# A two-layer decoder trunk with a searched order of issue: the order searched anew, the sinks' load on SyncE's queue, the first weight row in two transfers, and tile 0's output ahead of tile 1's

## The chip, the cores and the metric

The kernel runs on one core of one Trainium2 chip. The metric is the device time of one execution, in microseconds (us). The engines are called as in the profile: PE (TensorE matmul) with PEld (its weight loads), DVE (VectorE), ACT (ScalarE), POOL (GpSimd) and SP (SyncE, which here only issues transfers).

## The reference

256 tokens of width 1024 go through two layers and a last norm. Each layer is conditioned by a vector c: a shift, a scale and a gate come from it by a product with a matrix of 1024 x 3072.

```python
c_act = jax.nn.silu(c)
for layer in range(DEPTH):
    ada = jnp.einsum('bd,de->be', c_act, w_ada[layer]) + b_ada[layer]
    shift, scale, gate = jnp.split(ada, 3, axis=-1)
    h = rms_norm(x, norm_g[layer]) * (1.0 + scale[:, None, :]) + shift[:, None, :]
    ...
        y = even_mixer(h, w_in_even[i], w_out_even[i], a_sinks[i], ...)
        y = odd_mixer(h, w_in_odd[i], w_out_odd[i], cos, sin)
    x = x + gate[:, None, :] * y
return rms_norm(x, final_g)
```

Layer 0 (even) projects h to the heads of two attentions, one over a sliding window with a learned sink per head (`a_sinks`, eight numbers), one sparse in three branches. Layer 1 (odd) is a block-sparse attention. All is fp32.

## The kernel before

**Precision.** Each large product is made of three matmuls (`mm3`): both operands are split into a rounded part (hi) and a rest (lo), and hi x hi, hi x lo and lo x hi are added in PSUM. So each weight tile that lands in `raw` (a ring of five) is cast by ACT into `whi`, and DVE subtracts to get `wlo`; only then can PE use it. For the first layer `hhi`, `hlo` are the same two parts of the conditioned input h.

**Order.** No scheduler decides the order. Every call on an engine is first recorded by `Plan`, and then `issue` issues all of them in the order of a table, `ORDER` (3092 numbers in before, found by a search). Each engine works through its own calls in that order, and a call waits for what it depends on while all behind it on its engine wait too. A transfer's place in SP's order is thus its place in SP's queue. As all calls are issued at one line, every row of the profile shows L257, and operations are told apart by engine and tile.

**The opening.** The steps around the change, by their lines of before:

- The loads of x (`xs`, one transfer of 512 KB for each of two tiles of 128 tokens) and small tables; c comes in as `crow`, and `cz` holds its activated form, made on DVE out of `tiny`.
- The norm of x for each tile t, then eight transposes on PE, copied by DVE and ACT into `bigA` (`xT`).
- `start_ada` and `start_sums` (L710, L722). The weights of the projection are taken in eight rows of 128 of the 1024 inputs, and a row can begin when its shift and scale are known. So the conditioning matrix is read in pieces, for two rows at a time (`START`): eight transfers of 256 KB into the tiles `qT` (six) and `gate` (two) for rows 0 and 1, into the four tiles `t` for rows 2 and 3, and so on in turn. For the first pair PE sums all of it by 32 matmuls of 128 x 128 (`ps_m<-qT,cz` and `ps_m<-gate,cz`, two records each in the profile). For later pairs DVE sums a part (`acc`), and PE the rest (`ps_m<-t,cz`, `ps_m<-acc,ones`). ACT copies the sum (`asb`), PE transposes it, and two adds on DVE give `shs`.
- `start_row` (L767) loads a weight row into `raw`: 1304 columns (652 KB) and 384 columns (192 KB). `start_prep` (L773) makes `hhi` on ACT and `hlo` on DVE for this row and splits the weights. `start_mm` (L781) runs 24 matmuls for the row, 3 each of 512, 408, 512 and 256 columns for two token tiles, into seven PSUM banks that collect over all eight rows (`ps_s`, `ps_pj`, `ps_o`, `ps_pt`).
- The sinks (L814) are spread to 128 partitions, 32 bytes each, by one transfer of 4 KB on GpSimd's queue. DVE negates them; they are first used in an attention at 73 us. `rows` takes in `b_ada` and `norm_g`, also on GpSimd's queue; DVE needs them for `shs`.

**The middle** (from about 28 to 212 us) holds the other rows, the first layer's attentions with the conditioning of the rest, the output projection and the second layer's beginning.

**The tail.** The last product is made in pieces: columns 0 to 511 and then, for tile 0, the rest in one piece, for tile 1 in two. When a tile is complete, its norm is a root on ACT, a reciprocal on DVE, and two scalings into `t`: ACT's of 384 columns, sent from ACT's queue, and DVE's of 640, sent from SP's.

Of the kernel before, what the change touches and what calls it, by code (L numbers as in the profile page):

```python
# [13 lines left out]
P = 128  # L14
# [254 lines left out]
def tile_trunk(  # L269
# [24 lines left out]
    V, A, G, T, Y = plan.vector, plan.scalar, plan.gpsimd, plan.tensor, plan.sync  # L294
# [408 lines left out]
    W0 = w_in_even[0]  # L703
# [669 lines left out]
```

## Time and profile before

| what | value |
|---|---|
| time of a run: median of 3 (lowest to highest) | 306.07 us (305.75 to 307.39) |
| span of the profiled execution | 305.1 us |
| granted PE clock, mean | 0.997 |
| busy PE, DVE, ACT | 289.9, 260.4, 187.1 us |
| moved by transfers | 71.82 MB, mean 235 GB/s |

The span runs from the first to the last instruction of one execution; of that execution the profile gives no other time. A row of a timeline gives the start, the time, the engine, line and operation, the tiles as out<-in, the shape, how many were joined, and in brackets the idle time before it with what ended it. Rows with SPq, ACTq or POOL DMA are issues of transfers, not the transfers. Some tiles carry numbers in the order of issue (`qT0`, `qT1`) that the profile leaves out.

### The profile page before, as it was taken

The page shows a single profiled execution, that of the slowest core. Times are in us where ns is not written, and L with a number is a line of the kernel's source. Part 1 is how long each engine was busy: PE and PEld are TensorE (multiplying, and loading weights), DVE is VectorE, ACT ScalarE, POOL GpSimd, SP SyncE. Part 2 cuts the span into 40 slices and gives each one's busy share as a digit, 9 for nine tenths or more (in the row PEclk, how much of TensorE's full clock was granted, in tenths as well). Part 3 has the DMA queues.
Part 4 walks back from the last instruction along what each step waited for, and adds up shares of the span by engine and source line. Part 5 has one row for each costly group of instructions (what it writes and reads, how often), then busy time and mean ns, then how long its engine had stood idle before and what let it go on. Part 6 is the DMA issues. An engine that isn't in the chain of part 4 may idle for free.

```text
span 305.1 us, 6309 instructions
## 1 busy us (share of the span) xinstructions
PE 289.9 (95%) x2303; PEld 247.7 (81%) x2303; DVE 260.4 (85%) x706; ACT 187.1 (61%) x487; POOL 10.7 (4%) x34
## 2 busy tenths in 40 slices
PE   3969999999999999999999999999999999999991
PEld 2848888897888777877877799999789989887791
DVE  0377998999999999999999679697685999999983
ACT  4364446885687888974547753655376357685522
POOL 6000000001000000000011000000000000000010
PEclk9999999999999999999999999999999999999998
DMA  7999999989496668699799805948099673172003
GB/s 188 374 391 383 387 398 373 330 260 305 133 347 203 197 201 269 215 299 356 215 332 363 263 2 168 355 167 272 6 308 305 175 249 138 12 268 69 2 0 138
DMA packets 60669, 71.82 MB, mean 235 GB/s; under 512 B 2712, under 2 KB 52320, under 8 KB 60640
## 3 DMA queue, kind: packets, MB, share of 16 engines
q1 hardware_dynamic: 60032, 70.90, 69.7%
q0 software_dynamic: 160, 0.05, 0.5%
q10 hardware_dynamic: 448, 0.48, 0.4%
q8 instruction: 18, 0.29, 0.4%
q14 instruction: 11, 0.09, 0.1%
HBM read 70.38 MB, written 1.05 MB: 234 GB/s over the span
## 4 chain that ended last, share of the span: by engine, by line
PE 85%; DMA 9%; DVE 2%; ACT 1%; SPq 1%; issue 0%; ACTq 0%; DVEq 0%
PE ps_pj L257 51%; PE ps_s L257 12%; PE ps_o L257 7%; PE ps_pt L257 7%; PE ps_m L257 6%; DMA raw<-in_w_ada_dram 3%; DMA raw<-in_w_in_even_dram 3%; DMA qT<-in_w_ada_dram 2%; SPq L257 1%; DVE acc L257 1%; ACT whi L257 1%; DVE wlo L257 1%; ACT t L257 0%; DVE xs L257 0%; DVE sm L257 0%
## 5 line engine op out<-in xcount | busy, mean ns | idle before, releaser
L257 ACT CAST whi<-raw 128x512 fp32r<-128x512 f32 (+1 forms) x132 | 74.7, 600 | 34.9 <-PE ps_pj L257 17.5
L257 DVE TENSOR_TENSOR wlo<-raw,whi 128x512 fp32r<-128x512 f32 (+1 forms) x116 | 73.2, 659 | 3.6 <-ACT whi L257 3.2
L257 PE MATMUL ps_pj<-hlo,whi 128*128 128x256 f32 x256 | 71.8, 286 | 0.0
L257 PE MATMUL ps_pj<-hhi,wlo 128*128 128x256 f32 x256 | 71.7, 288 | 0.0
L257 PE MATMUL ps_pj<-hhi,whi 128*128 128x256 f32 x256 | 71.4, 290 | 0.1
L257 PEld LDWEIGHTS ps_pj<-hlo,whi 128*128 128x128 f32 x256 | 47.9, 188 | 2.2 <-issue 2.0
L257 PEld LDWEIGHTS ps_pj<-hhi,wlo 128*128 128x128 f32 x256 | 47.9, 189 | 0.6 <-issue 0.5
L257 PEld LDWEIGHTS ps_pj<-hhi,whi 128*128 128x128 f32 x256 | 47.3, 188 | 1.2 <-issue 0.6
L257 DVE SCALAR_TENSOR_TENSOR acc<-raw,cz,acc 128x512 f32<-128x512 f32 x42 | 31.4, 748 | 0.3
L257 ACT ACTIVATE sm<-sm,mn 128x128 f32<-128x128 f32 (+1 forms) x58 | 26.1, 452 | 5.6 <-DVE mn L257 5.6
L257 PE MATMUL ps_pj<-whi,hhi 128*128 128x512 f32 (+2 forms) x72 | 26.5, 381 | 1.5 <-ACT hhi L257 1.5
L257 DVE SCALAR_TENSOR_TENSOR wlo<-raw,whi 128x512 fp32r<-128x512 f32 x32 | 21.2, 686 | 7.7 <-ACT whi L257 7.7
L257 PE MATMUL ps_pj<-wlo,hhi 128*128 128x512 f32 (+2 forms) x72 | 26.6, 372 | 0.0
L257 PE MATMUL ps_pj<-whi,hlo 128*128 128x512 f32 (+2 forms) x72 | 26.3, 367 | 0.0
L257 PE MATMUL ps_pj<-whi,ghi 128*128 128x512 f32 (+1 forms) x56 | 20.8, 373 | 0.0
L257 PE MATMUL ps_pj<-wlo,ghi 128*128 128x512 f32 (+1 forms) x56 | 20.7, 370 | 0.0
L257 PE MATMUL ps_pj<-whi,glo 128*128 128x512 f32 (+1 forms) x56 | 20.4, 364 | 0.0
L257 ACT COPY pT<-ps_pt 128x384 f32<-128x384 f32 x25 | 11.9, 477 | 10.7 <-PE ps_pt L257 10.6
L257 PE MATMUL ps_pt<-ta,sm 128*128 128x128 f32 x87 | 18.4, 275 | 0.0
L257 PEld LDWEIGHTS ps_pj<-whi,hhi 128*128 128x128 f32 x72 | 13.3, 189 | 4.2 <-ACT hhi L257 2.0
L257 PEld LDWEIGHTS ps_pj<-wlo,hhi 128*128 128x128 f32 x72 | 13.6, 188 | 2.5 <-issue 0.4
L257 PEld LDWEIGHTS ps_pj<-whi,hlo 128*128 128x128 f32 x72 | 13.6, 189 | 2.0 <-DVE hlo L257 0.2
(235 smaller groups left out, 606.1 us busy)
## 6 DMA issues: line engine op xcount, KB each, us to landing
raw<-in_w_in_odd_dram SPq DMA_DIRECT2D x16, 1024.0 KB, 6.9
raw<-in_w_ada_dram SPq DMA_DIRECT2D x28, 512.0 KB, 6.9
raw<-in_w_in_even_dram SPq DMA_DIRECT2D x8, 652.0 KB, 7.2
raw<-in_w_in_even_dram SPq DMA_DIRECT2D x5, 1024.0 KB, 10.1
t<-in_w_ada_dram SPq DMA_DIRECT2D x16, 256.0 KB, 6.7
raw<-in_w_out_even_dram SPq DMA_DIRECT2D x4, 1024.0 KB, 6.2
raw<-in_w_out_odd_dram SPq DMA_DIRECT2D x4, 1024.0 KB, 7.0
qT<-in_w_ada_dram SPq DMA_DIRECT2D x12, 256.0 KB, 7.2
```

Source lines behind the costliest of these rows:

```text
L257: self.ops.append(dict(key=eng.key, deps=deps, fn=lambda: getattr(real, name)(*args, **kw)))
```

## The change

1. `ORDER` is another table, with 3093 numbers. Calls up to about 212 us stand in another order on each engine, displaced by some four places on PE and DVE in the mean; behind that both orders are the same up to the tail.
2. Row 0's transfer of 1304 columns is made as two, of 512 and 792 columns. The other rows keep one.
3. The sinks' load goes from GpSimd's queue to SP's.

```diff
 ORDER = [int(i) for i in """
-0 2 8 997 10 23 29 1 3 22 510 73 4 76 78 30 77 31 7 5 79 74 32 33 58 11 6 80 12 992 13 27 43 75 14 15 92 16 44
+0 2 8 3 78 74 998 993 73 10 4 58 59 5 22 11 1 23 76 80 6 32 511 29 31 75 79 77 12 7 60 28 62 25 26 61 83 24 30
...
     def start_row(g):
         raw = sb([P, 2048], "raw", RAW)
-        Y.dma_start(raw[:, 0:1304], W0[g * P : (g + 1) * P, 1152:2456])
+        for a, b in ((0, 512), (512, 1304)) if g == 0 else ((0, 1304),):
+            Y.dma_start(raw[:, a:b], W0[g * P : (g + 1) * P, 1152 + a : 1152 + b])
         Y.dma_start(raw[:, 1304:1688], W0[g * P : (g + 1) * P, 256:640])
...
     snk = const([P, 16], "snk")
-    G.dma_start(snk[:, 0:8], a_sinks[0:1, :].to_broadcast([P, 8]))
+    Y.dma_start(snk[:, 0:8], a_sinks[0:1, :].to_broadcast([P, 8]))
```

SP's queue in the opening, before: both tiles of x, the eight conditioning tiles of the first pair, then `raw0` (row 0) and `raw1` (row 1).

```order
L257 DMA xs_61<-in_x_dram 128x1024 x2
L257 DMA qT0_97<-in_w_ada_dram 128x2x256
L257 DMA qT1_98<-in_w_ada_dram 128x2x256
L257 DMA qT2_99<-in_w_ada_dram 128x2x256 x2
L257 DMA gate_76<-in_w_ada_dram 128x2x256
L257 DMA qT0_97<-in_w_ada_dram 128x2x256
L257 DMA gate_76<-in_w_ada_dram 128x2x256
L257 DMA qT1_98<-in_w_ada_dram 128x2x256
L257 DMA raw1_101<-in_w_in_even_dram 128x384
L257 DMA raw0_100<-in_w_in_even_dram 128x1304
L257 DMA raw0_100<-in_w_in_even_dram 128x384
L257 DMA raw1_101<-in_w_in_even_dram 128x1304
```

And now, from the second tile of x on; ahead of it stand the first tile of x and three conditioning tiles.

```order
L257 DMA xs_61<-in_x_dram 128x1024
L257 DMA qT1_98<-in_w_ada_dram 128x2x256
L257 DMA gate_76<-in_w_ada_dram 128x2x256
L257 DMA snk_116<-in_a_sinks_dram 128x8
L257 DMA qT1_98<-in_w_ada_dram 128x2x256
L257 DMA gate_76<-in_w_ada_dram 128x2x256
L257 DMA qT2_99<-in_w_ada_dram 128x2x256
L257 DMA raw0_100<-in_w_in_even_dram 128x384
L257 DMA raw0_100<-in_w_in_even_dram 128x792
L257 DMA t40_86<-in_w_ada_dram 128x2x256 x2
L257 DMA raw0_100<-in_w_in_even_dram 128x512
L257 DMA raw1_101<-in_w_in_even_dram 128x1304
```

The second tile of x stands behind three conditioning tiles, the sinks in the midst of them; row 0 comes ahead of row 1, its narrow columns first, and two tiles of the second pair's conditioning (`t40`) ahead of its first 512 columns.

PE in the opening, before: the sums of the first pair in one run, behind the last transposes of x, then row 0 (`whi_108`, `wlo_112` are its 1024 wide columns, `whi_109` the narrow ones; `whi_110` is of row 1).

```order
L257 MATMUL ps_s_91<-ta,t_87 128x128
L257 MATMUL ps_m_67<-qT_97,cz 32x128 x8
L257 MATMUL ps_m_67<-qT_98,cz 32x128 x8
L257 MATMUL ps_m_67<-qT_99,cz 32x128 x8
L257 MATMUL ps_m_67<-gate,cz 32x128 x8
L257 MATMUL ps_m_67<-ta,asb_106 128x128
L257 MATMUL ps_pj_94<-whi_108,hhi 128x512
...
L257 MATMUL ps_s_91<-whi_108,hlo 128x512
L257 MATMUL ps_s_90<-whi_110,hhi 128x512
L257 MATMUL ps_o_96<-whi_109,hhi 128x408
```

PE now, from the last sums that stand among the transposes of x on.

```order
L257 MATMUL ps_m_67<-qT_98,cz 32x128 x4
L257 MATMUL ps_s_90<-ta,t_87 128x128 x3
...
L257 MATMUL ps_pt_83<-ta,rows_pe 128x32
L257 MATMUL ps_m_67<-qT_99,cz 32x128 x4
L257 MATMUL ps_m_67<-gate,cz 32x128 x4
L257 MATMUL ps_s_91<-ta,t_87 128x128
L257 MATMUL ps_m_67<-ta,asb_106 128x128
L257 MATMUL ps_s_91<-ta,t_87 128x128
L257 MATMUL ps_pt_83<-whi_109,hhi 128x256
L257 MATMUL ps_o_96<-whi_109,hhi 128x408
```

24 of the 32 sums stand ahead, between the transposes, and eight behind them; `cz`, which they need, is DVE's fifth call now and stood tenth before. Row 0 begins with the narrow columns, and the first matmul of row 1 comes after 21 matmuls of row 0, where it came after 13.

ACT in the tail, before (`t_86` is tile 1's output here, `t_87` tile 0's; `parts<-parts` is the root, `t_88,parts<-xs` the square of a piece).

```order
L257 ACTIVATE parts<-parts 128x1
L257 ACTIVATE t_88,parts<-xs 128x256
L257 ACTIVATE parts<-parts 128x1
L257 ACTIVATE t_86<-xs,parts 128x384
L257 DMA out_dram<-t_86 128x384
L257 ACTIVATE t_87<-xs,parts 128x384
L257 DMA out_dram<-t_87 128x384
```

And now:

```order
L257 ACTIVATE parts<-parts 128x1
L257 ACTIVATE t_87<-xs,parts 128x384
L257 DMA out_dram<-t_87 128x384
L257 ACTIVATE t_88,parts<-xs 128x256
L257 ACTIVATE parts<-parts 128x1
L257 ACTIVATE t_86<-xs,parts 128x384
L257 DMA out_dram<-t_86 128x384
```

Tile 0's scaling and its transfer stand right behind tile 0's root, ahead of tile 1's last square, in place of the very end.

258 rows, old and new, of the table ORDER are left out of this document.

## The prediction

> **What bounds the kernel now.** I read the clock first, then the page's busy shares, the table by stretches, the chain of waits, and last the opening, one place of the middle and the tail instruction by instruction.
>
> ```profile
> core 0: 305.1 us, clock 0.997
> PE 289.9 (95%) x2303; PEld 247.7 (81%) x2303; DVE 260.4 (85%) x706; ACT 187.1 (61%) x487; POOL 10.7 (4%) x34
> 100.00:130.00 30.00, 30.00 (x273) 23.38 (x271) 29.03 (x110) 25.80 (x84) 0.00 (x0) 1.00 0.65 213
> ```
>
> The clock is full, so nothing is to be had there. The columns of a stretch are its length, then the busy time of PE, of its weight loads, DVE, ACT and POOL, the clock, the DMA share and GB/s. PE has no idle time in this one, and DVE is busy 97% of it. So in the middle neither engine has much to give, and time can be won only before that stage, by beginning it sooner, or after the last matmul. The chain of waits says the same: behind 21.7 us it is PE almost all the way, and ahead of it stand two transfers.
>
> ```profile
> PE 85%; DMA 9%; DVE 2%; ACT 1%; SPq 1%; issue 0%; ACTq 0%; DVEq 0%
> ...
> 3.38 7.24 DMA qT<-in_w_ada_dram
> ...
> 10.64 8.84 DMA raw<-in_w_in_even_dram
> ...
> 19.50 1.14 ACT whi L257 x2
> ```
>
> The profiled execution has a span of 305.1 us; the median of the three runs shown is 306.07, 0.97 above it. I make the sum as a difference to the span and put it on the median.
>
> **Opening: the sums and the first weight row.**
>
> ```profile
> 6.34 0.76 SPq L257 DMA_DIRECT2D qT<-in_w_ada_dram  x1
> DMA to landing us min/median/max: 6.8/7.3/7.7
> 13.18 1.60 PE L257 MATMUL ps_m<-qT,cz 128*32 128x128 f32 x48
> 14.60 0.62 PE L257 MATMUL ps_m<-gate,cz 128*32 128x128 f32 x16
> 15.31 0.27 ACT L257 COPY asb<-ps_m 128x128 f32<-128x128 f32 x1 [0.33 <-PE ps_m L257]
> 16.19 0.16 DVE L257 TENSOR_TENSOR shs<-shs,rT 128x2 f32<-128x2 f32 x1
> 16.82 0.60 ACT L257 ACTIVATE hhi<-bigA,shs 128x256 fp32r<-128x256 f32 x1
> 17.47 0.73 PE L257 MATMUL ps_pj<-whi,hhi 128*128 128x512 f32 x2 [1.51 <-ACT hhi L257]
> 21.70 0.49 PE L257 MATMUL ps_s<-whi,hhi 128*128 128x512 f32 x1 [1.06 <-ACT whi L257]
> ```
>
> The last of the eight conditioning tiles is issued at 6.34 us and, with the median of the qT loads, lands at about 13.6. Only then can the sums of the first two rows end, but PE begins all 64 of their matmul records at 13.18 and ends them at 15.22, 1.6 us behind the landing. The change interleaves them with the transposes of x as tiles land and leaves eight instructions for the end, shown in the order of issue as two rows of four; 64 records took 2.04 us, so a quarter of them is 0.5 us. That ends the sums 1.1 us sooner. Of the rest up to 17.47 (2.25 us: copy, transpose, two adds, hhi) nothing is removed; two weight casts on ACT stand ahead of hhi in both orders, now of the narrow columns that come first. I take 1.0 for the start of row 0, with bounds of 0.5 (ACT is late) and 1.5.
>
> Before, PE ran 13 of row 0's 24 matmuls, then waited 1.06 us at 21.70 for a cast of row 1's weights, of the transfer that the chain shows landing at 19.48. Now 21 of the 24 come first. They outlast that landing, so this wait goes: another 1.06 on PE. But the next thing is late then:
>
> ```profile
> 13.73 6.13 SPq L257 DMA_DIRECT2D t<-in_w_ada_dram  x5
> 20.61 0.34 SPq L257 DMA_DIRECT2D raw<-in_w_in_even_dram  x1
> L257 PE MATMUL ps_m<-t,cz x32: 272/273/297, 25.3 to 26.1; 128*32 128x128 f32 x32
> 27.45 0.69 DVE L257 TENSOR_TENSOR wlo<-raw,whi 128x512 fp32r<-128x512 f32 x1 [1.84 <-ACT whi L257]
> ```
>
> The second conditioning group needs its t tiles; the last is issued by 19.86, and with the shortest landing of the t loads (5.1, below) it lands at about 24.6. The group's matmuls began at 25.3, so they can begin at most about 0.7 sooner. Of the 2.06 won up to there the rest isn't all lost, since PE does matmuls of row 1 meanwhile that it has to do anyhow. Of DVE's wait of 1.84 (row 2's cast came behind asb on ACT) about half should go, and DVE is the engine without slack behind it. I take **-1.1** for the whole opening at equal transfer rate, nearer to the 0.7 than to the 2.06, and bounds of -0.3 (DVE holds it) and -2.1.
>
> ```profile
> DMA to landing us min/median/max: 5.1/8.2/8.4
> ```
>
> The first row's wide transfer becomes two, one issue more on SP. SP issues such a transfer in 0.34 us (20.61) and then mostly waits for landings, so I cost it at nothing; were SP late, it would be 0.34. Raw0's 512 columns now stand behind two t tiles, 512 KB; at the 396 GB/s quoted below 1.3 us. The 16 matmuls on the other columns that now come first cover that.
>
> **Opening: the sinks on SP's queue.**
>
> ```profile
> 1.35 0.71 POOL L257 DMA_DIRECT2D snk<-in_a_sinks_dram  x1
> 2.06 0.53 POOL L257 DMA_DIRECT2D rows<-in_b_ada_dram  x1
> DMA to landing us min/median/max: 6.2/6.2/6.2
> 4.00:5.00 1.00, 0.00 (x0) 0.00 (x0) 0.00 (x0) 0.60 (x1) 0.00 (x0) 1.00 1.01 396
> 5.00:6.00 1.00, 0.00 (x0) 0.00 (x0) 0.00 (x0) 0.81 (x3) 0.03 (x1) 1.00 1.68 77
> 6.00:7.00 1.00, 0.95 (x4) 0.96 (x5) 0.09 (x2) 0.88 (x2) 1.00 (x3) 1.00 0.35 80
> ```
>
> Between 5 and 7 us the transfers fall from 396 to 77 and 80 GB/s. That loses (2 x 396 - 157)/396 = 1.6 us of transfer, and the conditioning tiles, which the whole opening waits for, come 1.6 us later. The sinks land in that hole (1.35 + 6.2 = 7.5): 128 rows of 32 bytes, the first transfer on GpSimd's queue. The trace can't say whether the hole belongs to these short rows, to the first transfer of that queue, or to the sinks on that queue alone. In the first case it moves with them to SP's queue, in the second b_ada's rows inherit it, and in both the term is 0; in the third it is -1.6. I take 0, since two of three causes keep it, with -1.6 and +1.6 (both at once) as ends.
>
> The Trainium skill, "DMA: Bandwidth & Descriptors", section Specifications, puts the full rate at transfers of 512 bytes and up, with read-modify-write below; by that the hole belongs to the short rows and the term is 0. The same page, "Issuing engines are not separate DMA queues", says that a change of issuing engine saves only issue time; by that too it is 0. The hole is in this trace, its cause is not.
>
> GpSimd's other work (memsets, the pow of the norm) is off the chain, and has one issue of 0.71 less. DVE negates the sinks at place 8 of its queue now, ahead of the copies of x's transposes; if they landed as late as 13 us, everything behind would wait. They are the seventh transfer, so this costs nothing while they land by about 10.
>
> **Middle.** Up to 212 us the order differs, with the same work. What I can price is PE changing between kinds of matmul. The quadrant and single fp32 ones stand alone among the weight matmuls more often: I count 24 such quadrant runs instead of 20 and 35 fp32 runs instead of 28 in PE's first 1100 places.
>
> ```profile
> 86.85 0.30 PE L257 MATMUL ps_m<-kcbd,qT 128*128 128x32 f32 x2
> 86.98 0.36 PE L257 MATMUL ps_pj<-hhi,wlo 128*128 128x256 f32 x1
> 87.19 0.28 PE L257 MATMUL ps_pj<-hhi,whi 128*128 128x256 f32 x1
> 87.31 0.28 PE L257 MATMUL ps_pj<-hlo,whi 128*128 128x256 f32 x1
> 87.43 0.27 PE L257 MATMUL ps_pt<-ta,sm 128*128 128x128 f32 x1
> 87.63 0.93 PE L257 MATMUL ps_s<-kTb,qT 64*128 64x128 f32 x8
> 88.49 0.39 PE L257 MATMUL ps_pj<-hlo,whi 128*128 128x256 f32 x1
> 88.71 0.28 PE L257 MATMUL ps_pj<-hhi,wlo 128*128 128x256 f32 x1
> ```
>
> A weight matmul follows the one before by 0.12 (87.19 to 87.31). Behind the fp32 pair it is 0.21 (86.98 to 87.19): 0.09 for a run. Into the quadrant run it is 0.20 and out of it 0.22: about 0.18 over the pitch. So 4 x 0.18 + 7 x 0.09 = 1.35 us if PE never waits. Where PE now gets ahead of DVE part of it falls into waits. I take **+0.6**, between 0 and +1.35; what else a new order wins or loses in a stretch where both engines are full I can't see, and I allow it 0.5 either way.
>
> **Tail.**
>
> ```profile
> 297.35 0.42 ACT L257 ACTIVATE t<-xs 128x256 f32<-128x256 f32 x1 [2.28 <-DVE xs L257]
> 300.09 0.62 ACT L257 ACTIVATE t<-xs,parts 128x384 f32<-128x384 f32 x1 [0.33 <-DVE parts L257]
> 300.73 0.36 ACTq L257 DMA_DIRECT2D out_dram<-t  x1
> 301.79 0.35 ACTq L257 DMA_DIRECT2D out_dram<-t  x1
> DMA to landing us min/median/max: 2.1/2.4/2.6
> ```
>
> Tile 0's part of ACT (0.62 and an issue of 0.36) goes from the very end into the idle 2.28 us ahead of 297.35. It needs tile 0's reciprocal, then 1.0 us, so the square at 297.35 is late by 0.1 at most, which tile 1's later PE result covers. The last output is then the one issued at 300.73: with the longest landing 303.3, against 301.79 + 2.1 = 303.9 now. **-0.5**, bounds 0 and -1.06 (the issue times apart).
>
> Sum: -1.1 + 0 + 0.6 - 0.5 = -1.0, so 305.1 us.
>
> **The rivals.** *The hole vanishes*: everything of the opening comes another 1.6 us sooner, weights and t tiles alike; -2.6, 303.5. For it: the 0.05 MB of GpSimd's queue make a hole that no other transfer of the opening has. Against it: the two rules above, and that DVE, 97% busy behind it, may not let PE keep all.
> *The hole doubles*: b_ada's rows inherit one, the sinks on SP make a second, in the middle of the conditioning tiles; +1.6, 306.7. It decides if the tiles then land more than 1.1 us later than now.
> *The middle is slower*: the order that fills PE starves DVE once by as much as the 1.84 that it waits at 27.45, and the extra runs cost their full 1.35; DVE has 3% to make that up. -1.1 - 0.5 + 1.35 + 1.84 = +1.6, 307.7. It decides from +1.6 in the middle on, where opening and tail are used up. For it: casts, splits and scores of that stretch arrive just ahead of use. Against: a wait that long was seen only where a load had landed late.
>
> **How the numbers follow.** Chances: the sum as it stands 0.45, vanished hole 0.28, doubled 0.10, slower middle 0.17. A measurement here tells about 0.5% (1.53 us) from no change: faster is below 304.5, slower above 307.6. Faster: five sixths of the vanished hole and a third of the sum as it stands, 0.38. Slower: half of the slower middle and a third of the doubled hole, some 0.13. Same: 0.49. The range takes the vanished hole with 0.6 more, 302.9, and the slower middle up to 307.6; what lies outside is about 0.2. The likeliest case alone has 304.2 to 306.1.
>
> **What would show it.** Right: the sums end at about 14.1, row 0 starts at about 16.4, no wait of 1 us at 21, the second group's matmuls at about 24.6, the last output issued at about 300; a hole of 1.6 us in the transfers still there. The hole gone and the last conditioning tile at 12.0 would show the first rival; two holes the second; DVE idle for over 4 us between 28 and 170 the third. The forecast is wrong altogether if PE waits in the first 212 us longer than before.

## The result: slower by 1.3%

The changed kernel takes 310.59 us in the median of four runs (310.17 to 310.75), the kernel before 305.95 us in four runs beside it (305.75 to 307.39): a ratio of 1.0129 with an interval of 1.0094 to 1.0163. The forecast was 305.1 us with a range up to 307.6, so the time lies outside it, on the slow side. The profiled execution's span is 308.7 us against 305.1, so its trace shows 3.6 us of the difference. Two profiled executions further below were slow ones at a lower clock (327.54 us at 0.846 and 309.87 us at 0.985), so of the first no trace is read, and of the second only the opening.

```profile
core 0: 308.7 us, clock 0.993
```

First the busy shares and the stretches of the changed kernel, with the columns of those shown of before, then two stretches of before.

```profile
PE 297.9 (97%) x2303; PEld 252.9 (82%) x2303; DVE 260.6 (84%) x706; ACT 186.9 (61%) x487; POOL 10.5 (3%) x33
```

```profile
0.00:24.00 24.00, 19.99 (x143) 15.71 (x143) 11.31 (x31) 11.28 (x21) 5.47 (x23) 0.93 0.90 302
24.00:68.00 44.00, 43.28 (x324) 38.11 (x324) 38.66 (x84) 27.99 (x70) 0.53 (x1) 1.00 1.04 362
100.00:130.00 30.00, 30.00 (x258) 23.35 (x258) 28.18 (x110) 23.77 (x77) 0.00 (x0) 1.00 0.64 211
```

```profile
0.00:24.00 24.00, 15.62 (x134) 13.07 (x135) 9.93 (x27) 11.16 (x21) 5.46 (x21) 1.00 0.97 322
24.00:68.00 44.00, 44.00 (x331) 38.74 (x330) 40.47 (x89) 28.36 (x70) 0.55 (x2) 1.00 1.04 359
```

PE has the same 2303 instructions and is busy 8.0 us longer; 4.4 of them lie in the first 24 us, part of which it now runs at a lower clock. In the stretch of 100 to 130 us it is busy all the time, as before, but gets 258 instructions done where it got 273, and DVE fell from 29.03 to 28.18 us. So PE doesn't wait there; its own work has become longer. A busy share alone would have read as "better used".

Where the time comes from is seen by setting the start of the same instruction side by side in both traces:

| start of | before | after | difference |
|---|---|---|---|
| the second conditioning group (`ps_m<-t,cz`) | 25.3 | 24.0 | -1.3 |
| the first product of the sparse attention's compressed branch (`ps_m<-raw,t`) | 68.89 | 68.69 | -0.2 |
| the first compressed values (`ps_o<-pcT`) | 118.62 | 122.09 | +3.5 |
| the last square of the tail (ACT `t<-xs`) | 297.35 | 301.69 | +4.3 |
| end of the span | 305.1 | 308.7 | +3.6 |

The opening wins 1.3 us up to 24 us, most of it is gone at 68 us, the middle loses 4.5 us, and the tail wins 0.7. Each column is one execution, and executions scatter: of before and the kernels below, four executions with before's opening come to `ps_m<-raw,t` at 68.5 to 69.5 us, and those with before's order behind 120 us need 178.1 to 179.1 us from the first compressed values to the last square. So the 4.5 us are clear, and differences of some tenths are not.

**The middle.** PE's timeline at the group of scores that the prediction showed at 87.63 us, in the changed kernel:

```profile
88.52 0.92 PE L257 MATMUL ps_s<-kTb,qT 64*128 64x128 f32 x4
89.37 0.39 PE L257 MATMUL ps_pj<-hhi,whi 128*128 128x256 f32 x1
...
91.19 0.92 PE L257 MATMUL ps_s<-kTb,qT 64*128 64x128 f32 x4
92.04 0.39 PE L257 MATMUL ps_pj<-hhi,wlo 128*128 128x256 f32 x1
```

Before, eight records in one run held PE for 0.86 us (87.63 to 88.49). Now four of them hold it for 0.85 (88.52 to 89.37) and the other four again for 0.85 (91.19 to 92.04): 1.70. In the order of issue the eight records are four calls, two for `ps_s_90` and two for `ps_s_91`. Each call uses 64 of the 128 rows of the array (64*128 in the profile). Before:

```
L257 MATMUL ps_s_90<-kTb,qT_97 128x128
L257 MATMUL ps_s_91<-kTb,qT_97 128x128
L257 MATMUL ps_s_90<-kTb,qT_97 128x256
L257 MATMUL ps_s_91<-kTb,qT_97 128x256
```

And after, where thirteen other matmuls stand between the halves:

```
L257 MATMUL ps_s_90<-kTb,qT_97 128x128
L257 MATMUL ps_s_90<-kTb,qT_97 128x256
...
L257 MATMUL ps_s_91<-kTb,qT_97 128x128
L257 MATMUL ps_s_91<-kTb,qT_97 128x256
```

So the two halves of the array run at the same time when their matmuls stand together, and one half stands empty when they don't. The groups of the whole span show it. The first number behind the bar is the busy time, in which a stretch counts once however many matmuls run in it, the second the mean ns of one. Before:

```profile
L257 PE MATMUL ps_s<-kTb,qT 64*128 64x256 f32 x48 | 7.2, 377 | 0.0
L257 PE MATMUL ps_s<-kTb,qT 64*128 64x128 f32 x48 | 5.9, 323 | 0.0
```

After:

```profile
L257 PE MATMUL ps_s<-kTb,qT 64*128 64x256 f32 x48 | 8.9, 386 | 0.0
L257 PE MATMUL ps_s<-kTb,qT 64*128 64x128 f32 x48 | 7.9, 323 | 0.0
```

One matmul lasts about as long as before, there are as many, and the busy time has grown by 3.7 us: they overlap less. (The two rows also overlap each other, so 3.7 us is more than the loss; the starts below give 2.1 us for these groups.) The Trainium skill has this as a rule: "TensorEngine Tiling (Array Packing)", section Key Properties, says "Tiles operate independently: Different tiles can execute LdWeights and Matmul in parallel". This trace agrees, with 0.86 us together and 0.85 + 0.85 apart.

Worked out from the starts of the matmuls in both traces, four groups of scores are split: one by +0.84 us (88.5), and three, of which two of eight records stand apart, by +0.41 each (97.9, 113.9, 129.3). A group of values (`ps_o<-pT,vb`, at 100 to 103 us) is split by seven matmuls: 1.45 to 2.02, +0.57. In the run of 32 records of the compressed branch's first product, which use quarters of the array (128*32; the expectations below call them conditioning rows), the order inside has changed. Before and after:

```profile
68.89 2.15 PE L257 MATMUL ps_m<-raw,t 128*32 128x256 f32 x32
70.97 0.44 PE L257 MATMUL ps_pt<-ta,t 128*128 128x128 f32 x2
```

```profile
68.69 2.84 PE L257 MATMUL ps_m<-raw,t 128*32 128x256 f32 x32
71.46 0.39 PE L257 MATMUL ps_pj<-hhi,whi 128*128 128x256 f32 x1
```

That is 2.08 to 2.77 us, +0.69. Together 0.84 + 3 x 0.41 + 0.57 + 0.69 = 3.3 us of the 4.5.

**The opening.** PE's timeline of the changed kernel, then of before:

```profile
1.06 4.22 PE L257 MATMUL ps_m<-ones 128*128 128x128 f32 x22 [1.06 <-DVE ones L257]
...
7.75 1.35 PE L257 MATMUL ps_pj<-ta,t 128*128 128x128 f32 x5 [1.60 <-DVE t L257]
...
14.24 0.64 PE L257 MATMUL ps_m<-qT,cz 128*32 128x128 f32 x8
14.70 0.61 PE L257 MATMUL ps_m<-gate,cz 128*32 128x128 f32 x8
15.25 0.33 PE L257 MATMUL ps_s<-ta,t 128*128 128x128 f32 x1
...
17.10 0.39 PE L257 MATMUL ps_pt<-whi,hhi 128*128 128x256 f32 x1 [0.97 <-ACT hhi L257]
```

```profile
6.22 4.40 PE L257 MATMUL ps_m<-ones 128*128 128x128 f32 x22
10.46 0.27 PE L257 MATMUL ps_pj<-ta,t 128*128 128x128 f32 x1
```

The sums end at 15.25, not at 14.1 as forecast, and row 0 starts at 17.10, 0.37 sooner than before. The wait of 1.06 at 21.70 is gone, and the second group starts at 24.0. The 22 matmuls on `ones`, whose result nobody uses, show something that the prediction passed over. Before, they filled PE until the first transposes; now they stand ahead of the first wait, and PE idles 1.60 us just ahead of the transposes. In that idle time its clock falls to half (the mean from 7 to 8 us is 0.82), and it returns at 11 us, as the stretches of the changed kernel show (clock in the column before the last two):

```profile
8.00:9.00 1.00, 1.00 (x5) 0.70 (x4) 0.34 (x2) 0.00 (x0) 0.13 (x1) 0.50 1.06 375
9.00:10.00 1.00, 1.00 (x13) 0.58 (x12) 0.00 (x0) 0.95 (x1) 0.00 (x0) 0.50 0.91 295
10.00:11.00 1.00, 1.00 (x8) 0.48 (x6) 0.15 (x1) 0.19 (x2) 0.54 (x1) 0.50 1.01 331
...
17.00:18.00 1.00, 0.90 (x6) 0.90 (x7) 0.90 (x3) 1.00 (x4) 0.00 (x0) 1.00 0.78 240
18.00:19.00 1.00, 1.00 (x8) 0.89 (x7) 1.00 (x3) 1.00 (x3) 0.00 (x0) 1.00 0.67 199
```

The last two rows show the transfers at 240 and 199 GB/s where before they ran at 362. SP stood then behind PE's transposes of tile 0, which free the tile that its next transfer fills (SP's waits up to 40 us: sum, count, longest):

```profile
SPq L257 <- PE ps_s L257: 3.6, 2, 3.2
```

Later, PE waits once for the conditioned input of a row, which it didn't before:

```profile
39.41 0.73 PE L257 MATMUL ps_pj<-whi,hhi 128*128 128x512 f32 x2 [0.72 <-ACT hhi L257]
```

**The tail.**

```profile
299.64 0.62 ACT L257 ACTIVATE t<-xs,parts 128x384 f32<-128x384 f32 x1 [0.23 <-DVE parts L257]
300.29 0.35 ACTq L257 DMA_DIRECT2D out_dram<-t  x1
...
301.69 0.42 ACT L257 ACTIVATE t<-xs 128x256 f32<-128x256 f32 x1 [1.43 <-DVE xs L257]
...
305.07 0.36 ACTq L257 DMA_DIRECT2D out_dram<-t  x1
```

Tile 0's scaling and its transfer lie in the idle time ahead of the square. From the square to the last issue are 3.38 us now, and were 4.44 (297.35 to 301.79); to the end of the span 7.0, and were 7.75.

### The profile page after: what moved, and what is told of

The parts are those of the page before. It is cut to its first block, busy times and chain, and to the rows that moved or that the text cites. A ratio compares the mean times of both kernels' runs of the same rounds, so it can differ in the third digit from the quotient of the medians.

```text
span 308.7 us, 6292 instructions
## 1 busy us (share of the span) xinstructions
PE 297.9 (97%) x2303; PEld 252.9 (82%) x2303; DVE 260.6 (84%) x706; ACT 186.9 (61%) x487; POOL 10.5 (3%) x33
## 4 chain that ended last, share of the span: by engine, by line
PE 88%; DMA 6%; SPq 2%; ACT 1%; DVE 1%; POOL 0%; issue 0%; ACTq 0%; POOLq 0%; DVEq 0%
PE ps_pj L257 55%; PE ps_s L257 12%; PE ps_m L257 8%; PE ps_o L257 7%; PE ps_pt L257 7%; DMA raw<-in_w_in_even_dram 3%; DMA qT<-in_w_ada_dram 2%; SPq L257 2%; DMA ta<-in_tbl_a_dram 1%; ACT whi L257 0%; DVE t L257 0%; DVE xs L257 0%; ACT t L257 0%; ACTq L257 0%; POOL r L257 0%
## 5 line engine op out<-in xcount | busy, mean ns | idle before, releaser
L257 ACT CAST whi<-raw 128x512 fp32r<-128x512 f32 (+1 forms) x132 | 73.9, 599 | 26.6 <-PE ps_pj L257 16.9
L257 PE MATMUL ps_pj<-hhi,wlo 128*128 128x256 f32 x256 | 69.5, 289 | 0.0
L257 PE MATMUL ps_pj<-hlo,whi 128*128 128x256 f32 x256 | 69.4, 287 | 0.0
L257 PEld LDWEIGHTS ps_pj<-hhi,wlo 128*128 128x128 f32 x256 | 46.9, 188 | 1.7 <-issue 1.1
L257 PEld LDWEIGHTS ps_pj<-hlo,whi 128*128 128x128 f32 x256 | 46.7, 188 | 1.4 <-issue 1.1
L257 ACT ACTIVATE sm<-sm,mn 128x256 f32<-128x256 f32 (+1 forms) x58 | 25.9, 449 | 3.5 <-DVE mn L257 3.5
L257 PE MATMUL ps_pj<-whi,hhi 128*128 128x512 f32 (+2 forms) x72 | 25.4, 373 | 0.7 <-ACT hhi L257 0.7
L257 DVE TENSOR_TENSOR t<-ps_pj,tb 128x512 f32<-128x512 f32 (+2 forms) x22 | 11.9, 585 | 5.7 <-PE ps_pj L257 5.6
L257 ACT ACTIVATE whi<-raw 128x512 fp32r<-128x512 f32 x16 | 9.9, 631 | 9.4 <-PE ps_pj L257 7.5
```

The costliest lines, as they stand in the source:

```text
L257: self.ops.append(dict(key=eng.key, deps=deps, fn=lambda: getattr(real, name)(*args, **kw)))
```

## The experiments

**Theory A**: the loss is in PE's own time; groups of matmuls that use halves or quarters of the array lose their overlap when the order splits them. **Rival B**: it is what the prediction feared, entries and exits of more short runs, and waits that follow from a later opening; then the groups of the array's parts cost little. For the rest: that the tail and the opening are worth what was forecast, and whose the hole in the transfers is. The kernels are named by their edit. Rows of these kernels say L258 or L259 where the text is one or two lines longer. Before ran beside them on each of three chips, with medians of 307.07 us (the order inside the groups, the first gathering, the tail, opening and tail), 306.24 (the split, the sinks alone, sinks and tail, the second tile of x) and 306.05 (the rest). A ratio is estimated from the runs that it compares, so it isn't exactly the quotient of two medians.

**Groups split in the kernel before.** In before, four of the groups of scores are split, the second half's two matmuls four places later; 28 places of PE's order change, no other engine's.

```diff
 MATMUL ps_s_90<-kTb,qT_97 128x128
-MATMUL ps_s_91<-kTb,qT_97 128x128
 MATMUL ps_s_90<-kTb,qT_97 128x256
-MATMUL ps_s_91<-kTb,qT_97 128x256
 MATMUL ps_pj_92<-hlo,whi_111 128x256
 MATMUL ps_pj_92<-hhi,wlo_115 128x256
 MATMUL ps_pt_83<-ta,sm_125 128x128 x2
+MATMUL ps_s_91<-kTb,qT_97 128x128
+MATMUL ps_s_91<-kTb,qT_97 128x256
```

> The kernel before with four of its twelve window score groups split: the two matmuls of one half of the array stay, the two of the other half come four weight matmuls later. 28 places of PE change, nothing on another engine. Theory A, narrowed to split groups (the halves no longer run side by side): the changed kernel's trace has a group so split at 1.70 us where before has 0.86, so 4 x 0.84 = 3.4 us more, 1.1%. Theory B (a kind change costs 0.2 to 0.3 a run, the halves don't matter): 0.8 to 1.2 more, 0.3 to 0.4%.

Measured: 310.13 us, ratio 1.0113 (1.0074 to 1.0153) to 306.24 of before on the same chip; span 308.3. PE's timeline at one of the four:

```profile
83.48 0.92 PE L258 MATMUL ps_s<-kTb,qT 64*128 64x128 f32 x4
84.33 0.38 PE L258 MATMUL ps_pj<-hlo,whi 128*128 128x256 f32 x1
...
84.98 0.92 PE L258 MATMUL ps_s<-kTb,qT 64*128 64x128 f32 x4
85.83 0.39 PE L258 MATMUL ps_pj<-hhi,wlo 128*128 128x256 f32 x1
```

Each half holds PE for 0.85 us alone, each group costs 0.84 more, four of them 3.4 us. That is A's number, and B's 0.3 to 0.4% lies outside the interval. It is the cost of the split itself: all other calls keep their order.

**Only the order inside the groups.** In before, the groups stay together but get the changed kernel's order inside.

```diff
 MATMUL ps_s_90<-kTb,qT_98 128x128
-MATMUL ps_s_91<-kTb,qT_98 128x128
 MATMUL ps_s_90<-kTb,qT_98 128x256
+MATMUL ps_s_91<-kTb,qT_98 128x128
 MATMUL ps_s_91<-kTb,qT_98 128x256
...
-MATMUL ps_m_67<-raw_102,t_87 32x256 x2
-MATMUL ps_m_67<-raw_101,t_87 32x256 x2
...
+MATMUL ps_m_67<-raw_101,t_87 32x256 x8
+MATMUL ps_m_67<-raw_102,t_87 32x256 x8
```

> The kernel before, its order untouched but for the order inside the same quadrant groups, which is the changed kernel's (for scores half 0 twice and then half 1 twice). No group is split, no kind change added. Theory A: 2 to 3 us more than before, 308 to 309. Theory B and C: no change, 306.0.

Measured: 307.79 us, ratio 1.0032 (1.0 to 1.0065) to 307.07 of before on the same chip; span 306.1. This expectation of A missed. The groups of scores still take 0.86 us each; only the run over quarters grew, as in the changed kernel:

```profile
68.74 2.85 PE L258 MATMUL ps_m<-raw,t 128*32 128x256 f32 x32 [0.28 <-issue]
```

So A has to be narrowed. Over halves, two calls of the same half in a row cost nothing: in the seven groups so ordered, the other half's first matmul starts 0.013 us behind the first one (0.007 before), 0.31 us ahead of the first half's second call, which stands before it in PE's order. The loss comes when other work stands between. Over quarters, eight calls on two of them ahead of the eight on the other two do cost 0.7 us. All 16 of these calls write one PSUM bank and still overlap in before, so separate banks, which the halves have, aren't what the overlap needs.

**The groups gathered in the changed kernel.** The changed kernel, with the groups of the middle put back together in before's order inside, all else as it is.

```diff
 MATMUL ps_s_90<-kTb,qT_97 128x128
+MATMUL ps_s_91<-kTb,qT_97 128x128
 MATMUL ps_s_90<-kTb,qT_97 128x256
+MATMUL ps_s_91<-kTb,qT_97 128x256
...
-MATMUL ps_s_91<-kTb,qT_97 128x128
-MATMUL ps_s_91<-kTb,qT_97 128x256
```

> The changed kernel, with the matmuls of each quadrant group of the middle (scores, sparse values, conditioning rows from raw) put side by side again in before's inner order; all else is the new order. Theory A (the new order breaks the interleaving of matmuls on different halves or quarters of the array, so they run one behind another): 3.0 to 3.9 us less than the changed kernel, 306.7 to 307.6. Theory B (only the number of changes between kinds of matmul counts): at most 0.6 less, 310.0. Theory C (DVE and ACT results come too late in the new order): no change, or longer, since some groups now wait for their last operand.

Measured: 307.49 us, ratio 1.0026 (1.0 to 1.0051). The trace of this run isn't read, for the clock named above. The same kernel was run again, beside the changed kernel on one chip:

> The first run's kernel again (the changed kernel with its quadrant groups put together), for a trace of it and a time beside the changed kernel's on the same chip. Theory A: its five split groups fall from 7.5 to 4.9 us of PE in the trace and the conditioning rows from 2.77 to 2.08, 3.3 us in all; 3.0 to 3.6 less than the changed kernel. Rest of the middle (kind changes, later waits): 1.0 to 1.5 above the third run.

> The changed kernel as it is, once more, on the chip of the three other runs of this call, so that they can be compared with it directly: 1.0 to 1.6% above before, 310 to 311.

Measured: the changed kernel 310.47 us, ratio 1.0119 (1.008 to 1.0157), span 308.5; gathered 307.23 us, ratio 1.0016 (0.9989 to 1.0042), span 305.0. Gathering gives back 3.2 us by the runs and 3.5 by the spans, against the 3.3 worked out above. PE's timeline of the gathered kernel:

```profile
68.88 2.05 PE L259 MATMUL ps_m<-raw,t 128*32 128x256 f32 x32 [0.70 <-issue]
...
89.47 0.93 PE L259 MATMUL ps_s<-kTb,qT 64*128 64x128 f32 x8
90.33 0.39 PE L259 MATMUL ps_pj<-hhi,wlo 128*128 128x256 f32 x1
...
118.81 0.65 PE L259 MATMUL ps_o<-pcT,vz 128*64 128x256 f32 x4
```

The group is at 0.86 us again, and the first compressed values start at 118.81 in place of 122.09. A is shown from both sides. What is left of the middle in the changed kernel (4.54 less 3.34), +0.75 us up to there and about +0.45 behind it, is in no one place, and the latter is within the scatter named above. Waits are no part of it: from 68.70 to 300 us PE is busy all of the 231.30 us. By the tiles, PE goes 234 times between weight matmuls, other whole-array matmuls and matmuls on parts of the array from the first of these points to the last square, in before 205 times. So the price that the prediction named is of the size of the rest, but no run isolates it.

**The tail alone.** Before, with ACT's five calls of the tail in the changed order.

```diff
 ACTIVATE parts<-parts 128x1
+ACTIVATE t_87<-xs,parts 128x384
+DMA out_dram<-t_87 128x384
 ACTIVATE t_88,parts<-xs 128x256
 ACTIVATE parts<-parts 128x1
 ACTIVATE t_86<-xs,parts 128x384
 DMA out_dram<-t_86 128x384
-ACTIVATE t_87<-xs,parts 128x384
-DMA out_dram<-t_87 128x384
```

> The kernel before with only tile 0's scaling and output on ACT put ahead of tile 1's last square. As forecast: 0.5 less (0 to 1.06), 305.4; by the changed kernel's trace, whose lag falls by 0.7 over the tail, 305.3. If the end is set by SP's output of tile 1 instead: no change.

Measured: 306.5 us, ratio 1.0 (0.9967 to 1.0032): not resolved by the runs. The timeline does show the tail:

```profile
298.25 0.42 ACT L258 ACTIVATE t<-xs 128x256 f32<-128x256 f32 x1 [1.43 <-DVE xs L258]
...
301.64 0.36 ACTq L258 DMA_DIRECT2D out_dram<-t  x1
```

This execution came to the square 0.9 us later than before's and ended its span only 0.4 later: 7.25 us from square to end in place of 7.75. In seven other profiled executions with this tail, the changed kernel's among them, it is 6.95 to 7.02, in three others without it 7.73 to 7.76. So the tail is worth 0.5 to 0.8 us.

**Opening and tail of the changed kernel, middle of before.** The changed order up to PE's place 120, and from there before's, but for the tail.

```diff
 MATMUL ps_pj_92<-wlo_115,hhi 128x408
+MATMUL ps_s_90<-wlo_114,hhi 128x512
+MATMUL ps_s_90<-whi_110,hlo 128x512
+MATMUL ps_pj_92<-whi_111,hlo 128x408
 MATMUL ps_pt_83<-whi_111,hlo 128x256
-MATMUL ps_s_91<-wlo_114,hhi 128x512
 MATMUL ps_m_67<-ta,asb_107 128x128
```

> The opening of the changed kernel (up to the second pair's sums, with the sinks on SP's queue and the split transfer) and its tail, with the middle in before's order. If the loss is all in the middle: the opening's 1.2 us and the tail's 0.6 remain, 304.2. If the opening's gain is given back at the next late load whatever follows: 305.4 (tail alone). If the opening loses by its clock drop at 8 to 11 us: above 306.

Measured: 306.05 us, ratio 0.9969 (0.9944 to 0.9995), about -0.95 us; span 303.5. Its second conditioning group starts at 23.8, 1.5 us sooner than before's, but at the first `ps_m<-raw,t` only 0.14 us are left. Of the span's 1.6 us the tail gives 0.8, and 0.65 come between 150 and 245 us, where both kernels have one order: that is scatter. So the order of the opening is worth little, though it does win its time at first.

**Two transfers moved back in SP's queue.** The same kernel, with the two transfers for which SP waits behind the next four.

```diff
-DMA t_87<-in_w_ada_dram 128x2x256 x2
 DMA t_88<-in_w_ada_dram 128x2x256
 DMA t_89<-in_w_ada_dram 128x2x256
 DMA t_88<-in_w_ada_dram 128x2x256
 DMA t_89<-in_w_ada_dram 128x2x256
+DMA t_87<-in_w_ada_dram 128x2x256 x2
```

> The third run's kernel (opening and tail of the changed kernel) with the two transfers into the second pair's tile that tile 0's transposes must free put behind the four others on SP's queue. Theory (the opening's gain is lost where SP stands 2.3 to 3.2 us behind these transposes): that wait goes, rates at 17 to 22 us come back to 360 to 390 GB/s, the first rows come 0.7 to 1.0 sooner than in the third run and the time is 0.5 to 0.7% below before. Rival (the clock drop and the transfers' total hold it): as the third run, 0.3% below.

Measured: 305.16 us, ratio 0.9961 (0.9936 to 0.9987), span 303.4. The transfers run through:

```profile
17.00:18.00 1.00, 0.74 (x5) 0.74 (x6) 0.90 (x3) 1.00 (x3) 0.00 (x0) 1.00 0.96 358
18.00:19.00 1.00, 1.00 (x8) 0.89 (x7) 1.00 (x3) 1.00 (x3) 0.00 (x0) 1.00 1.08 384
```

But the next thing is late then, a sum that DVE makes:

```profile
25.70 0.30 PE L258 MATMUL ps_m<-acc,ones 128*32 128x128 f32 x1 [0.47 <-DVE acc L258]
```

It is 0.26 us ahead of before from 36 us on, where the kernel without this edit is about 0.15 ahead from 40 us on; their intervals overlap almost wholly. So SP's wait was real and cost next to nothing.

**The second tile of x back in second place.** The kernel of opening and tail again, with x loaded first as in before.

```diff
-DMA xs<-in_x_dram 128x1024
+DMA xs<-in_x_dram 128x1024 x2
 DMA qT<-in_w_ada_dram 128x2x256
 DMA qT<-in_w_ada_dram 128x2x256 x2
-DMA xs<-in_x_dram 128x1024
 DMA qT<-in_w_ada_dram 128x2x256
```

> The kernel of the third run (opening and tail of the changed kernel, middle of before) with the second tile of x second in SP's queue again instead of fifth. Theory: x's late tile makes its transposes late, which free the buffers of the second pair's conditioning tiles; SP stood 3.2 us behind that, and the transfers fell to 199 to 311 GB/s at 17 to 22 us. Then this wait goes, the second and third groups' tiles land 1.0 to 1.5 earlier and the time falls by as much against the third run: 0.7 to 0.8% below before. Rival: the opening is held by something else behind 30 us (DVE or the rate of the transfers): same as the third run, 0.3% below before.

Measured: 306.69 us, ratio 0.9995 (0.9967 to 1.0024), span 306.8. The expected gain of 0.7 to 0.8% didn't come; it lies outside the interval. Why, the trace can't say, since in this profiled execution the clock stayed at half to beyond 17 us:

```profile
16.00:17.00 1.00, 1.00 (x6) 0.93 (x5) 0.00 (x0) 0.00 (x0) 0.00 (x0) 0.50 0.96 387
```

SP then waited 7.1 us for the same transposes. So moving x forward isn't enough by itself, and this opening is open to the clock.

**The sinks on SP's queue alone.** Before, with one transfer moved.

```diff
-    G.dma_start(snk[:, 0:8], a_sinks[0:1, :].to_broadcast([P, 8]))
+    Y.dma_start(snk[:, 0:8], a_sinks[0:1, :].to_broadcast([P, 8]))
```

> The kernel before with only the sinks' load on SP's queue, between the seventh and the eighth transfer. If the hole of 1.6 us at 5 to 7 us belongs to the sinks on GpSimd's queue (rival one of the prediction): the last conditioning tile lands at 12.1 instead of 13.65 and the time falls by 1 to 1.6, 0.3 to 0.5%. If it goes with the short rows: no hole at 5, one of 1.6 a few us later, no change. If b_ada's load inherits it: no change or worse.

Measured: 306.47 us, ratio 0.9991 (0.9962 to 1.002). The stretches show what became of the hole (GB/s is the last column):

```profile
5.00:6.00 1.00, 0.00 (x0) 0.00 (x0) 0.00 (x0) 0.75 (x3) 0.00 (x0) 1.00 1.02 330
...
9.00:10.00 1.00, 1.00 (x8) 1.00 (x8) 0.52 (x3) 0.40 (x1) 0.00 (x0) 1.00 0.22 54
10.00:11.00 1.00, 1.00 (x11) 1.00 (x10) 0.00 (x0) 0.00 (x0) 0.00 (x0) 1.00 0.86 282
```

It has gone along with the sinks, from 5 to 7 us to 9 to 11. By the prediction's sum it loses (2 x 396 - 336)/396 = 1.15 us there, where it lost 1.6. This execution is 1.0 us ahead of before's from 24 us to 150 us and ends 1.6 ahead (span 303.5), but the runs don't show it.

**The sinks later, and the tail.** Before, with the tail and the sinks on SP's queue behind the loads of the first projection, their negation right ahead of its first use.

```diff
 DMA raw<-in_w_in_even_dram 128x8x256
 DMA raw<-in_w_in_even_dram 128x8x256
+DMA snk<-in_a_sinks_dram 128x8
 DMA raw<-in_cmp_w_k_dram 128x8x256
```

> The kernel before with the sinks' load on SP's queue behind the loads of the first projection (issued at about 48 us, where the queue waits for free buffers anyway), their negation on DVE right ahead of the first use, and the changed kernel's tail. Theory (the hole goes with the 128 short rows, whichever queue, and costs where transfers are the limit): no hole in the first 45 us; 1.6 us from the hole and 0.5 from the tail, 0.6 to 0.8% below before. If the hole comes from the first use of GpSimd's queue: it stays at 5 to 7 us, and only the tail's 0.5 remain.

Measured: 305.58 us, ratio 0.9975 (0.9943 to 1.0007). Of its trace the opening:

```profile
5.00:6.00 1.00, 0.00 (x0) 0.00 (x0) 0.00 (x0) 0.66 (x3) 0.00 (x0) 1.00 0.95 303
...
9.00:10.00 1.00, 1.00 (x7) 1.00 (x6) 0.48 (x3) 0.36 (x1) 0.00 (x0) 1.00 1.09 383
```

No hole is left in the opening, and `b_ada`'s rows, now first on GpSimd's queue, make none. So the hole goes with the sinks' transfer and not with a queue. Two things set this transfer apart: its 128 rows have 32 bytes, and all of them read the same 32. In before a load that spreads one row of 4 KB to 128 partitions (`gate<-in_b_ada`, 81.15 to 87.7 us) makes none, with 301 to 360 GB/s from 84 us to its landing, so the short rows are the likelier cause, but no run separates the two. The gain is less than the 0.6 to 0.8% expected, and one over the next kernel isn't resolved.

**The sinks on SP's queue and the tail.** Before, with these two edits shown above and nothing else.

```diff
-    G.dma_start(snk[:, 0:8], a_sinks[0:1, :].to_broadcast([P, 8]))
+    Y.dma_start(snk[:, 0:8], a_sinks[0:1, :].to_broadcast([P, 8]))
...
+ACTIVATE t_87<-xs,parts 128x384
+DMA out_dram<-t_87 128x384
 ACTIVATE t_88,parts<-xs 128x256
```

> The kernel before with the sinks on SP's queue and the changed kernel's tail, nothing else. The sum of the two alone: tail 0.5, hole 0 to 1.6, so 0.5 to 2.1 less (0.2 to 0.7%).

Measured: 304.95 us, ratio 0.9965 (0.9934 to 0.9997), span 302.7. This beats both kernels, the one before by about 0.35%, with an interval that just leaves out no change. The kernel with SP's two transfers moved back does as well (0.9961); the runs can't rank the two.

## Why the prediction was wrong

**The middle: the step that failed.** The prediction said "What I can price is PE changing between kinds of matmul" and took +0.6, with +1.35 as the end and 0.5 for what it couldn't see. The trace shows +4.5 from 68.7 us to the last square, of which 3.3 are the groups that lost their overlap. The step counted how many runs of the array's parts there are, 24 for 20, and priced the entry and the exit of each. It took for granted that what stands inside a run costs the same wherever the run is cut. The row quoted for that price in the prediction, eight records of `64*128` in 0.86 us, was the very group that came apart: its shape says that each call fills half of the array, and the row of its group, here 48 matmuls of 377 ns each in 7.2 us of busy time, that several run at once. Had the four more runs been traced to the groups that they were cut from, each whole group cut would have stood in the sum with another 0.86. The other price was about right in kind: some 1.2 us of the middle are left for entries and exits, within its end of +1.35, and PE doesn't wait there.

**The opening.** -1.1 for the whole was too much; about -0.2 is left at 68.7 us, less than the scatter of single executions. Forecast was row 0 at 16.4, measured 17.10. The eight last sums waited for PE to work off the transposes of tile 0: they start at 14.24, almost 1 us behind the last conditioning tile's landing at about 13.3. Half of the clock played a part, but not the greater one: in the kernel of opening and tail the clock stayed full, and row 0 started at 16.82. The second group came at 24.0, earlier than the 24.6 forecast, and the wait at 21 us was gone, as said. That 1.3 us shrink to 0.2 behind it is close to the prediction's bound of -0.3 ("DVE holds it"), just beyond it. Why they do is not settled: the transfers ran at 302 GB/s up to 24 us, where before's ran at 322, and are full from 24 to 68 us (a share of 1.04, as in before), but to bring the rate back won nothing that could be measured; DVE was late next. One thing the table hides: the two kernels with before's opening and only the sinks moved reach `ps_m<-raw,t` at 67.8 and 67.9 us, five executions with the changed opening, which moves them too (one with two further transfers moved), at 68.6 to 68.9. So in these traces the new order and the split transfer rather cost some 0.8 us of what the sinks give than win time.

**The sinks.** The term 0 held in the measure of the runs, and its reason is now shown: the hole goes with this transfer, whichever queue issues it, and vanishes from the opening with it. That agrees with both sections of the Trainium skill that the prediction named. But the hole of 1.6 us that was to be "still there" isn't: it lost 1.15 us with the sinks alone on SP's queue, and in five executions of the changed opening 0.35 to 0.8 by the same sum (0.4 in the rows above, 295 and 331 GB/s). With the traces' 1.0 us, the move may be worth some tenths or more. The first rival, that the hole belongs to the sinks on GpSimd's queue alone, is out.

**The tail.** -0.5 was right within its bounds; the traces give 0.5 to 0.8.

**The rivals.** The "slower middle" had the right sign and place, but not the mechanism: DVE wasn't starved for PE to wait, PE's work itself grew. DVE does idle more, 28.18 of 30 us busy where it was 29.03, but that is a result: PE has no idle time in that stretch for which DVE could be the cause.

The sum as measured: opening -0.2, sinks in it, middle +4.5, tail -0.7, together +3.6 of the span.

## What to carry to other kernels

Before moving matmuls, look at the tile shape in the profile's rows: calls of 64*128, 128*64 or 128*32 that stand side by side on different parts of the array share its time, so a group of them is to be priced as one piece and not cut. A search over orders needs that in its costs: a group of scores cut in two halves of the array cost its 0.85 us twice here. And on the engine that bounds the kernel, compare the start of the same instruction in both traces, not busy shares: PE's rose from 95% to 97% with the kernel getting slower.

## What the runs showed of the hardware beyond that

- The clock halved in a short idle time. In the 1.60 us ahead of 7.75 it fell, and it was at 0.50 from 8 to 11 us, in the second profile of the changed kernel too; around an idle time of 0.86 us, in the kernel of opening and tail, it stayed at 1.00. The two executions differ in more than that: there the 22 matmuls on `ones` had taken 5.07 us, here 4.22. The Trainium skill, "TensorE: Matmul & The Clock Gate", Part 1, names an idle window of about 3.4 us for that; here PE had run matmuls up to 6.2 us, so a shorter one did it. Where the border lies, no run here shows.
- Beside a transfer of 4 KB in 128 rows of 32 bytes, all from one source, the transfers' rate fell from 396 to 77 and 80 GB/s over two microseconds on GpSimd's queue, and to 54 and 282 on SP's; in the changed kernel, on SP's too, only to 295 and 331.
- The order inside a group over the halves of the array cost nothing (0.86 us either way, since the other half's matmul started 0.31 us ahead of one that stood before it in the order), while over its quarters eight and eight in place of two and two cost 0.7 us of 2.1.
